# One encoder layer on one core: rows and attention outputs loaded by GpSimd, first loads of a scan by shares, a chain of small operations marked urgent

## The chip, the core and the metric

The kernel runs on one core of a Trainium2 chip. The metric is the time of one execution on the device in microseconds (us). TensorE (PE in the profile) does the matrix products, VectorE (DVE), ScalarE (ACT) and GpSimd (POOL) the elementwise work, and SyncE (SP) sends transfers; sixteen DMA engines carry them out.

## The reference

One layer of a bidirectional encoder is applied to two inputs with shared weights: a prompt of 1024 tokens (A in this document and in the names that end in `_a`) and a sample of 512 (B, `_b`), each 1024 wide, in float32.

- h = RMSNorm(x), and one product h @ w_in gives the columns for all that follows.
- The mLSTM branch has 4 heads of 256, with q and k after a short convolution and SiLU. In chunks of 128 positions, forwards and backwards, a state C is carried: num = (q k^T with decay weights) v + q C, and the head's output is num / max(|den|, exp(-m)). The two directions are added, normed by head and multiplied by two gates.
- The attention branch has 3 groups (window and dilation 128/1, 512/4, 2048/16) of 8 heads of 64. The groups' outputs are mixed by their softmax denominators and gated.
- merged = sigmoid(g_A) (y_A @ w_proj_m) + sigmoid(g_B) (y_B @ w_proj_a); out = merged @ w_out; y = x + RMSNorm(out).

## The kernel before

Every float32 operand is split into a rounded high part and the rest, the low part, and every product is three matmuls: high x high, low x high, high x low (lines 188 to 196 of the profile). A *dense step* is such a triple with 512 columns. A dense product (tile `dense`) is a unit of several steps into one PSUM bank; its weights come as a 512 KB load into one of two places (`wraw0`, `wraw1`), and are split by ScalarE (high, `wh`) and VectorE (low, `wl`).

The values and most projections of the prompt come first, up to 1056 us. From there on the rest of the dense units is the *fill*, laid between the steps of four stages whose own work has long chains of small operations:

1. the mLSTM of the prompt (`mlstm`, with `core` for one chunk's sums), from 1056 to about 1345 us,
2. the attention of the prompt (`attend`), to about 1655,
3. the mLSTM of the sample (`mlstm_short`), to about 1834, with the prompt's mix of the attention groups (`combine`) beside it,
4. the attention of the sample (`attend` again, with T.n = 4), to about 2122. Its fill is, among other things, `branches` and `final`: the merge and the output product of the prompt.

Then come the sample's `combine` with `final` of the prompt's second half, and the sample's `branches` and `final`.

A stage says how many fill steps go to one *share*; `fill(x)` issues x shares at that place in the program. TensorE's and SyncE's instructions run in the order in which the program writes them. Those of VectorE, ScalarE and GpSimd are put in an order by a scheduler, before the run, by what is ready and by priority; each engine then runs its own list strictly in order.

Nearly all transfers are sent by SyncE. Loads can be `queue`d; each `tick` of a stage sends `pace` of them, which `spread(n)` sets so that the queue is empty after n ticks; `need` sends all that are left of a group; `fetch` (line 229) sends a load at once, after the stores that it depends on; `flush` sends stores and weight loads that wait for their tick.

What the change touches:

- `core` (lines 949 to 1000): for each chunk and direction, a product `num` in PSUM; VectorE takes the maximum and the reciprocal (`r`); in the first half of the chunks ScalarE then writes `num` x `r` to the head's sums (`X` in the profile, L990), in the second half VectorE adds it (L993). That frees the bank for the next `num`.
- the start of `mlstm`: loads of Q, K and the gate rows, V and G at once, then `lead` = 4 shares of fill, then the first products `a` of Q and K (L892).
- `attend` for the sample: in each of 12 problems the next one's loads (q|k into Q0 and V1a, v, bias) are queued and spread over 3 ticks (T.n - 1).
- `split` (lines 1588 to 1604): the normed rows of a branch (`ym`), 128x512 each, 36 in all, go into five places in turn (`sraw`, `ymr0` to `ymr3`), and each is split by ScalarE (L1603) and GpSimd (L1604) into high and low part.
- `combine`: loads of the attention outputs (`og`, three groups for each of four row blocks of the sample, into V0a and V1a) and of the gate (`az`, into X1, Q0, az0, az1); VectorE computes the weights `cw` from the denominators (L1523 to L1533).
- `ot`: the places from which attention outputs are stored to `og`, six in the sample's attention.

GpSimd sends no transfer in this kernel. The kernel is built with `dynamic_dma_scratch_size=1024`.

Of the kernel before, what the change touches and what calls it, by code (L numbers as in the profile page):

```python
# [22 lines left out]
F32 = mybir.dt.float32  # L23
F32R = mybir.dt.float32r
AF = mybir.ActivationFunctionType
# [4 lines left out]
P = 128  # L30
# [145 lines left out]
class Net:  # L176
# [51 lines left out]

    def fetch(self, key, out, src):
        self.flush(lambda p: p[1] == key)  # L230
        return self.nc.sync.dma_start(out, src)

# [624 lines left out]
    def mlstm(self, T, fill, steps, first, banks, lead, after, beside=()):  # L857
# [10 lines left out]
        with ExitStack() as stack:  # L868
# [80 lines left out]
            def core(k):  # L949
# [23 lines left out]
                if i < n - 1:  # L973
                    e = P - 1 if d == 0 else 0
                    if i == 0:
                        cf = sb.tile([P, 2, 258], F32, name=f"cf{d}", bufs=1)
                        nc.vector.tensor_copy(cf, pc[:, :, :258])
                    else:
                        cf = C[d][0]
                        nc.vector.scalar_tensor_tensor(cf, cf, rw[:, 1, e:e + 1], pc[:, :, :258], op0=OP.mult, op1=OP.add)  # L980
                    ch = sb.tile([P, 2, 258], F32R, name=f"ch{d}", bufs=1)
                    cl = sb.tile([P, 2, 258], F32R, name=f"cl{d}", bufs=1)
                    nc.scalar.activation(ch, cf, AF.Copy)
                    nc.vector.tensor_sub(cl, cf, ch.bitcast(F32))
                    C[d] = (cf, ch, cl)
                r = sb.tile([P, 4], F32, name="r", bufs=4)
                nc.vector.tensor_scalar(r[:, 1:2], pn[:, 256:257], m["fl"], pn[:, 257:258], op0=OP.max, op1=OP.max)
                nc.vector.reciprocal(r[:, 2:3], r[:, 1:2])
                if i < n // 2:
                    nc.scalar.activation(hacc[:, c], pn[:, :256], AF.Copy, scale=r[:, 2:3])  # L990
                    return
                hs = hacc[:, c]
                nc.vector.scalar_tensor_tensor(hs, pn[:, :256], r[:, 2:3], hs, op0=OP.mult, op1=OP.add)  # L993
                hn = hn_of()
# [16 lines left out]
            def load_G(h):  # L1011
                for c in range(2):
                    self.queue(("G", h), ("G", S, 2 * h + c), G[:, c], T.G[2 * h + c])

            self.need(("qk", 0))
            for d in range(2):
                rows(0, d)
            self.need(("v", 0))
            load_G(0)
            fill(lead)  # L1020
            for _ in prepare(0):
# [82 lines left out]
    def mlstm_short(self, T, fill, steps, first, banks, lead, after, beside=()):  # L1104
# [11 lines left out]
        with ExitStack() as stack:  # L1116
# [10 lines left out]
            G = [x0[:, 2 * S * i:2 * S * (i + 1)].rearrange("p (c s) -> p c s", c=2) for i in range(2)]  # L1127
            fill.stage(steps, lead + 2 * len(rounds) + 3)

# [87 lines left out]
            weigh(1)  # L1217
            fill(1)
            next(beside, None)
# [212 lines left out]
    def attend(self, T, fill, steps, first, banks, outs, after=None, beside=None, at=()):  # L1432
# [5 lines left out]
        with ExitStack() as st:  # L1438
# [26 lines left out]
            for i in range(12):  # L1465
                now = coming
                for j, t in enumerate(now):
                    if j == 1:
                        if i < 11:
                            coming = ready(i + 1)  # L1470
                            self.spread(T.n - 1)
                        elif after:
                            after()
                            self.spread(T.n + 1)
                    self.tick()
                    if j == 0:
                        self.need(("att", i))
                    if j == 1:
                        self.need(("table", i))
                        self.later.pop(i, lambda: None)()  # L1480
                    tiles.append(t)
                    self.att_round(tiles, fill)
                    if len(tiles) in at:
                        next(beside, None)
# [18 lines left out]
    def combine(self, T, bank, cs, ys, sb, azs, slow):  # L1503
# [8 lines left out]
        def load(t):  # L1512
            for g in range(3):
                self.fetch(("og", T.S), cs[t % 2][:, g], T.og[g, :, t * P:(t + 1) * P].rearrange("h t w -> t h w"))

# [41 lines left out]

        load(0)
        yield
        az, w = {}, []  # L1560
        for t in range(T.n):
            az[t] = az_of()
            self.fetch(("az", T.S), az[t].rearrange("p (c s) -> p c s", c=4), T.az[:, :, t * P:(t + 1) * P].rearrange("c p s -> p c s"))
            if t + 1 < T.n:
                load(t + 1)
# [5 lines left out]
            if not slow:  # L1571
                yield
                yield
            if t > 0:
# [13 lines left out]
    def split(self, T, b, row, places, halves):  # L1588
# [6 lines left out]
        for i in range(m + 3):  # L1595
            if i < m:
                t = self.rows_in.pop(0)
                self.rows_in.append(t)
                got.append(t)
                self.fetch(("ym", T.S, min((row + i) // 2, 4)), t, T.ym[row + i, :, b * BLK:(b + 1) * BLK])  # L1600
            if i >= 3:
# [156 lines left out]
def body(tc, a):  # L1758
# [3 lines left out]
    with ExitStack() as st:  # L1762
# [192 lines left out]
        with ExitStack() as s1:  # L1955
# [36 lines left out]
            with ExitStack() as s2:  # L1992
# [4 lines left out]
                head = N.ml_load(A, 0)  # L1997
                N.mlstm(A, fill, STEPS[0], head, ("a", "num", "kv"), 4,
                        hold("qkv", lambda: N.att_first(A)))
# [24 lines left out]
            nc.sync.dma_start(N.postw, a["postw"][0:1].to_broadcast([P, D]))  # L2024
            N.attend(B, fill, STEPS[3], kept["qkv"], ("lg", "o", "pt"), 6)
            end = N.pool(s1, "end", 1, "right")
# [71 lines left out]
```

## Time and profile before

| | |
|---|---|
| runs | 2277.78 us median of 3 (2277.17 to 2277.89) |
| the profiled execution's own time | 2278.09 us |
| its span | 2276.3 us |
| granted TensorE clock over the span | 0.995 |
| busy: TensorE, VectorE, ScalarE, GpSimd | 98%, 64%, 48%, 27% of the span |
| moved by DMA | 425.05 MB, 187 GB/s on average |

A line of the profile names the engine, the line of the kernel, the operation and its tiles (output<-inputs, buffer numbers left out); what stands in brackets at its end is the idle time of that engine just before, and what ended it. "PEclk" is the clock that TensorE was granted, with 1.00 for full speed.

### The profile page before, as it was taken

How to read it: one execution, taken by the hardware profiler on the slowest of the kernel's cores; microseconds unless marked ns; L12 is line 12 of the kernel's file. 1: busy time of each engine (PE TensorE's matmuls, PEld its weight loads, DVE VectorE, ACT ScalarE, POOL GpSimd, SP SyncE). 2: the span in 40 equal slices, each digit the busy share in tenths (PEclk: the TensorE clock that was granted, in tenths of full speed). 3: DMA queues.
4: the chain of work that ended last, by engine and by line, in shares of the span. 5: the costliest groups of instructions: out<-in, count | busy, mean ns of one | idle time of the engine just before them, and what ended most of it. 6: DMA issues, size and time to landing. Idle time of an engine off the chain costs nothing. (4 is left out here: it accounts for less than half of the span.)

```text
span 2276.3 us, 35152 instructions
## 1 busy us (share of the span) xinstructions
PE 2235.5 (98%) x12210; PEld 1951.7 (86%) x12210; DVE 1467.8 (64%) x2777; ACT 1100.5 (48%) x2255; POOL 623.6 (27%) x801
## 2 busy tenths in 40 slices
PE   9999999999999999999999999999999999999998
PEld 9999998888887888887888889989888878888787
DVE  5587556767899655643787776675477744556563
ACT  7444223434444433334677766676644354544332
POOL 1000023333333322222567640001033321311311
PEclk9999999999999999999999999999999999999999
DMA  9556435555332223424666559988788888787673
GB/s 355 192 138 143 117 113 194 196 193 195 118 111 101 95 82 109 146 97 159 242 214 218 157 164 250 237 234 216 203 240 264 250 259 221 192 261 208 219 248 116
DMA packets 253627, 425.05 MB, mean 187 GB/s; under 512 B 26209, under 2 KB 150753, under 8 KB 252681
## 3 DMA queue, kind: packets, MB, share of 16 engines
q1 hardware_dynamic: 249848, 410.20, 58.7%
q10 hardware_dynamic: 3600, 12.59, 1.4%
q8 instruction: 97, 1.59, 0.3%
q14 instruction: 82, 0.66, 0.1%
HBM read 302.72 MB, written 128.37 MB: 189 GB/s over the span
## 5 line engine op out<-in xcount | busy, mean ns | idle before, releaser
L194 PE MATMUL dense<-H,wh 128*128 128x512 f32 x672 | 280.5, 417 | 0.0
L196 PE MATMUL dense<-H,wl 128*128 128x512 f32 x672 | 265.6, 395 | 0.5 <-DVE wl L253 0.5
L195 PE MATMUL dense<-H,wh 128*128 128x512 f32 x672 | 264.5, 394 | 0.0
L196 PE MATMUL d<-Hh,phla 128*128 128x512 f32 x608 | 237.4, 390 | 2.2 <-DVE phla L538 2.2
L194 PE MATMUL d<-Hh,phla 128*128 128x512 f32 x608 | 236.9, 390 | 0.0
L195 PE MATMUL d<-Hl,phla 128*128 128x512 f32 x608 | 236.8, 390 | 0.0
L195 PE MATMUL d<-vlo,Hh 128*128 128x322 f32 x704 | 220.4, 313 | 0.8 <-DVE vlo L384 0.8
L196 PE MATMUL d<-vhi,Hl 128*128 128x322 f32 x704 | 220.3, 313 | 0.0
L194 PE MATMUL d<-vhi,Hh 128*128 128x322 f32 x704 | 220.3, 313 | 0.0
L253 DVE TENSOR_TENSOR wl<-wraw,wh 128x1024 fp32r<-128x1024 f32 x109 | 137.0, 1257 | 89.8 <-ACT wh L252 87.7
L556 POOL TENSOR_TENSOR psum_w<-pw_raw 128x512 f32<-128x512 f32 x38 | 57.5, 1512 | 445.8 <-DMA pw_raw<-w_in 422.1
L1399 DVE CUSTOM_DVE_ANT_0 ls<-lg,bias 128x256 f32<-128x256 f32 (+1 forms) x288 | 93.7, 362 | 132.7 <-PE lg L1387 68.2
L194 PE MATMUL d<-Hh,phlb 128*128 128x512 f32 x456 | 177.6, 390 | 0.0
L196 PE MATMUL d<-Hh,phlb 128*128 128x512 f32 x456 | 177.6, 389 | 0.0
L195 PE MATMUL d<-Hl,phlb 128*128 128x512 f32 x456 | 177.6, 389 | 0.0
L1403 ACT ACTIVATE ls<-ls,nm 128x256 f32<-128x256 f32 (+1 forms) x288 | 129.9, 453 | 79.6 <-DVE nm L1401 63.1
L252 ACT ACTIVATE wh<-wraw 128x1024 fp32r<-128x1024 f32 x110 | 116.0, 1054 | 85.1 <-DMA wraw<-w_pm 32.8
L196 PEld LDWEIGHTS dense<-H,wl 128*128 128x128 f32 x672 | 126.7, 189 | 29.7 <-DVE wl L253 0.9
L195 PEld LDWEIGHTS dense<-H,wh 128*128 128x128 f32 x672 | 127.8, 190 | 13.6
L194 PEld LDWEIGHTS dense<-H,wh 128*128 128x128 f32 x672 | 127.4, 190 | 13.5
L196 PEld LDWEIGHTS d<-Hh,phla 128*128 128x128 f32 x608 | 114.1, 188 | 27.6 <-DVE phla L538 4.2
L195 PEld LDWEIGHTS d<-vlo,Hh 128*128 128x128 f32 x704 | 133.5, 190 | 1.5 <-DVE vlo L384 1.4
(556 smaller groups left out, 5722.2 us busy)
## 6 DMA issues: line engine op xcount, KB each, us to landing
pw_raw<-w_in SPq DMA_DIRECT2D x76, 512.0 KB
wraw<-w_in SPq DMA_DIRECT2D x76, 512.0 KB
aqk_a<-pwk SPq DMA_DIRECT2D x48, 512.0 KB
aqk_b<-sw SPq DMA_DIRECT2D x48, 256.0 KB
wraw<-w_pm SPq DMA_DIRECT2D x24, 512.0 KB
wraw<-w_out SPq DMA_DIRECT2D x24, 512.0 KB
vb<-w_vp SPq DMA_DIRECT2D x16, 644.0 KB
va<-w_vp SPq DMA_DIRECT2D x14, 644.0 KB
```

The costliest lines, as they stand in the source:

```text
L194: nc.tensor.matmul(out, lh, rh, start=start, stop=False)
L195: nc.tensor.matmul(out, lh, rl, start=False, stop=False)
L196: nc.tensor.matmul(out, ll, rh, start=False, stop=stop)
L252: self.splits = (nc.scalar.activation(hi[:, :n], raw[:, :n], AF.Copy), on.tensor_sub(lo[:, :n], raw[:, :n], hi[:, :n].bitcast(F32)))
L253: on.tensor_sub(lo[:, :n], raw[:, :n], hi[:, :n].bitcast(F32)))
L556: self.nc.gpsimd.tensor_add(s[:, 0], ws[1][:, 0], ws[1][:, 1])
L1399: nc.vector.tensor_tensor_reduce(out=ls[:, hh], in0=ts["lg"][hh], in1=bt[:, hh], scale=1.0, scalar=NEG, op0=OP.add, op1=OP.max, accum_out= ...
L1403: nc.scalar.activation(ls[:, hh], ls[:, hh], AF.Exp, bias=nm[:, hh:hh + 1], accum_out=ot[:, 128 + hh:129 + hh])
```

## The change

1. `fetch` can send on another engine's queue. The rows of `ym` in `split`, and the sample's `og` and `az` loads in `combine`, are sent by GpSimd: 36 + 12 + 4 = 52 loads leave SyncE.
2. The sample's `combine` sends the loads of its second row block at its very start, and those of block t + 2 after block t.
3. At the start of `mlstm` the weight load that waits for its tick is sent first, and V and G are no longer sent before the fill; `lead` is 6, and the six shares come one by one, each with a tick that sends some of the queued loads.
4. In `core` the maximum, the reciprocal and the operation that takes `num` out of its bank are marked as of high priority, and the low part of the state (`cl`) is issued after them.
5. `mlstm_short` has one more share, of fill ahead of its first sums.
6. In the sample's attention the loads of the second problem are all sent at one tick.
7. Ten places `ot` instead of six.

The number of instructions of every kind on every engine is the same but for the 52 loads. In the new file lines stand 1 to 14 lower (L990 of before is L991, L1604 is L1618, L1672 is L1686).

SyncE at the start of the sample's attention, before (Q0 and V1a take q and k of the next problem, `sraw` and `ymr` rows for `split`, `wraw` weights):

```order
L2024 DMA postw_18375<-postw 128x1024
L210 DMA wraw1_8707<-w_in 128x1024
L231 DMA sraw_8777<-ym_a_70 128x512
L231 DMA ymr0_18367<-ym_a_70 128x512
L231 DMA Q0_18005<-aqk_b_75 64x512 x2
L231 DMA V1a_18426<-aqk_b_75 64x512 x3
L210 DMA wraw0_8706<-w_pm 128x1024
L231 DMA ymr1_18368<-ym_a_70 128x512
L210 DMA wraw1_8707<-w_pm 128x1024
L231 DMA ymr2_18369<-ym_a_70 128x512
L231 DMA V1a_18426<-aqk_b_75 64x512
```

and now:

```order
L2038 DMA postw_18375<-postw 128x1024
L210 DMA wraw1_8707<-w_in 128x1024
L231 DMA Q0_18011<-aqk_b_75 64x512 x2
L231 DMA V1a_18430<-aqk_b_75 64x512 x4
L231 DMA Q0_18011<-aqk_b_75 64x512 x2
L231 DMA V1a_18430<-aqk_b_75 64x512 x4
L231 DMA bias2_8768<-erep_3048 128x256 x2
L210 DMA wraw0_8706<-w_pm 128x1024
```

All loads of the second problem now stand ahead of the next weights, and the rows are gone from this queue.

GpSimd at the end of the sample's attention, before (H3 are low parts of the merged rows `mg`, L1672; V1b and K1 those of the rows of the sample; `ss` is the norm of an output row):

```order
L1672 TENSOR_TENSOR H3_19607<-mg_20869,H2_19606 128x512
L1672 TENSOR_TENSOR H3_19607<-mg_20891,H2_19606 128x512
L1604 TENSOR_TENSOR V1b_20944<-ymr3_18370,V0b_20943 128x512
L1604 TENSOR_TENSOR V1b_20944<-sraw_8777,V0b_20943 128x512
L1672 TENSOR_TENSOR H3_19607<-mg_20931,H2_19606 128x512
L1604 TENSOR_TENSOR V1b_20944<-ymr0_18367,V0b_20943 128x512
```

and now:

```order
L1686 TENSOR_TENSOR H3_19611<-mg_20873,H2_19610 128x512
L231 DMA V1a_21083<-og_b_81 128x4x132 x2
L231 DMA Q0_21085<-az_b_77 128x4x128
L1686 TENSOR_TENSOR H3_19611<-mg_20895,H2_19610 128x512
L1618 TENSOR_TENSOR V1b_20948<-ymr3_18370,V0b_20947 128x512
L1618 TENSOR_TENSOR V1b_20948<-sraw_8777,V0b_20947 128x512
L1618 TENSOR_TENSOR V1b_20948<-ymr0_18367,V0b_20947 128x512
L1618 TENSOR_TENSOR V1b_20948<-ymr1_18368,V0b_20947 128x512
L1686 TENSOR_TENSOR H3_19611<-mg_20935,H2_19610 128x512
L1618 TENSOR_TENSOR K1_20950<-ymr2_18369,K0_20949 128x512
L231 DMA ymr3_18370<-ym_b_80 128x512
L231 DMA sraw_8777<-ym_b_80 128x512
```

The two loads into V1a wait until the last attention product has read it; the last two merged low parts and three row loads (the third, into `ymr0`, is the next row) stand behind them.

ScalarE in the prompt's mLSTM, at the second chunk, before (`rm` are decay weights, `qh`, `kh`, `ch` high parts, X the head's sums):

```order
L926 ACTIVATE rm_9174<-rm_9174,col1024_382 128x128
L926 ACTIVATE rm_9232<-rm_9232,col1024_382 128x128
L938 ACTIVATE qh_9186<-qw_9184 128x256
L983 ACTIVATE ch1_9161<-cf1_9035 128x516
L990 ACTIVATE X0_8806<-num_9079,r_9110 128x256
```

and now:

```order
L983 ACTIVATE ch0_9121<-cf0_9004 128x516
L926 ACTIVATE rm_9195<-rm_9195,col1024_382 128x128
L252 ACTIVATE wh0_8708<-wraw0_8706 128x1024
L991 ACTIVATE X0_8806<-num_9100,r_9124 128x256
L641 ACTIVATE sw2_8775<-dense_9000 128x512
```

X has left the second `rm` and two high parts behind it, and a weight split has come ahead of it.

The diff:

```diff
--- before.py
+++ after.py
@@ -226,9 +226,9 @@
         while any(g == group for g, _ in self.queued):
             self.fetch(*self.queued.pop(0)[1])
 
-    def fetch(self, key, out, src):
+    def fetch(self, key, out, src, queue=None):
         self.flush(lambda p: p[1] == key)
-        return self.nc.sync.dma_start(out, src)
+        return (queue or self.nc.sync).dma_start(out, src)
 
     def take(self, name, dt=F32R, cols=2048):
 
@@ -981,16 +981,21 @@
                     ch = sb.tile([P, 2, 258], F32R, name=f"ch{d}", bufs=1)
                     cl = sb.tile([P, 2, 258], F32R, name=f"cl{d}", bufs=1)
                     nc.scalar.activation(ch, cf, AF.Copy)
-                    nc.vector.tensor_sub(cl, cf, ch.bitcast(F32))
                     C[d] = (cf, ch, cl)
                 r = sb.tile([P, 4], F32, name="r", bufs=4)
-                nc.vector.tensor_scalar(r[:, 1:2], pn[:, 256:257], m["fl"], pn[:, 257:258], op0=OP.max, op1=OP.max)
-                nc.vector.reciprocal(r[:, 2:3], r[:, 1:2])
+                hs = hacc[:, c]
+                with self.tc.high_priority():
+                    nc.vector.tensor_scalar(r[:, 1:2], pn[:, 256:257], m["fl"], pn[:, 257:258], op0=OP.max, op1=OP.max)
+                    last = nc.vector.reciprocal(r[:, 2:3], r[:, 1:2])
+                    if i < n // 2:
+                        nc.scalar.activation(hs, pn[:, :256], AF.Copy, scale=r[:, 2:3])
+                    else:
+                        last = nc.vector.scalar_tensor_tensor(hs, pn[:, :256], r[:, 2:3], hs, op0=OP.mult, op1=OP.add)
+                if i < n - 1:
+                    with self.tc.issue_after(last.ins):
+                        nc.vector.tensor_sub(cl, cf, ch.bitcast(F32))
                 if i < n // 2:
-                    nc.scalar.activation(hacc[:, c], pn[:, :256], AF.Copy, scale=r[:, 2:3])
                     return
-                hs = hacc[:, c]
-                nc.vector.scalar_tensor_tensor(hs, pn[:, :256], r[:, 2:3], hs, op0=OP.mult, op1=OP.add)
                 hn = hn_of()
                 nc.scalar.activation(hn, hs, AF.Square, accum_out=r[:, 0:1])
                 nc.gpsimd.tensor_scalar(r[:, 1:2], r[:, 0:1], 16.0 / 256, 16 * EPS, op0=OP.mult, op1=OP.add)
@@ -1012,12 +1017,15 @@
                 for c in range(2):
                     self.queue(("G", h), ("G", S, 2 * h + c), G[:, c], T.G[2 * h + c])
 
+            self.flush(lambda p: p[1][0] == "w")
             self.need(("qk", 0))
             for d in range(2):
                 rows(0, d)
-            self.need(("v", 0))
             load_G(0)
-            fill(lead)
+            self.spread(lead)
+            for _ in range(lead):
+                self.tick()
+                fill(1)
             for _ in prepare(0):
                 fill(1 / 3)
             front(0)
@@ -1125,7 +1133,7 @@
             ym_of = Rot(self, [sb.tile([P, 256], F32, name=f"ym{i}", bufs=1) for i in range(3)])
             x0 = self.take("X0", F32)
             G = [x0[:, 2 * S * i:2 * S * (i + 1)].rearrange("p (c s) -> p c s", c=2) for i in range(2)]
-            fill.stage(steps, lead + 2 * len(rounds) + 3)
+            fill.stage(steps, lead + 2 * len(rounds) + 4)
 
             def rows(h):
                 for d in range(2):
@@ -1215,7 +1223,7 @@
             next(beside, None)
             front(0)
             weigh(1)
-            fill(1)
+            fill(2)
             next(beside, None)
             for k, (h, i) in enumerate(rounds):
                 self.tick()
@@ -1468,7 +1476,7 @@
                     if j == 1:
                         if i < 11:
                             coming = ready(i + 1)
-                            self.spread(T.n - 1)
+                            self.spread(T.n - 1 if i or T.n > 4 else 1)
                         elif after:
                             after()
                             self.spread(T.n + 1)
@@ -1511,7 +1519,8 @@
 
         def load(t):
             for g in range(3):
-                self.fetch(("og", T.S), cs[t % 2][:, g], T.og[g, :, t * P:(t + 1) * P].rearrange("h t w -> t h w"))
+                self.fetch(("og", T.S), cs[t % 2][:, g], T.og[g, :, t * P:(t + 1) * P].rearrange("h t w -> t h w"),
+                           None if slow else nc.gpsimd)
 
         by = lambda x: x.rearrange("p g (a b) -> p g a b", a=4)
 
@@ -1556,12 +1565,15 @@
             self.put(("ym", T.S, 4), T.ym[8:12, :, t * P:(t + 1) * P].rearrange("c p s -> p c s"), ya, az)
 
         load(0)
+        if not slow:
+            load(1)
         yield
         az, w = {}, []
         for t in range(T.n):
             az[t] = az_of()
-            self.fetch(("az", T.S), az[t].rearrange("p (c s) -> p c s", c=4), T.az[:, :, t * P:(t + 1) * P].rearrange("c p s -> p c s"))
-            if t + 1 < T.n:
+            self.fetch(("az", T.S), az[t].rearrange("p (c s) -> p c s", c=4), T.az[:, :, t * P:(t + 1) * P].rearrange("c p s -> p c s"),
+                       None if slow else nc.gpsimd)
+            if slow and t + 1 < T.n:
                 load(t + 1)
             for step in (lambda: w.append(weigh(t)), lambda: mix(t, w[t]), lambda: add(t)):
                 with self.tc.issue_after(self.splits[0].ins), self.tc.issue_after(self.splits[1].ins):
@@ -1570,6 +1582,8 @@
                     yield
             if not slow:
                 yield
+                if t + 2 < T.n:
+                    load(t + 2)
                 yield
             if t > 0:
                 turn(t - 1, az[t - 1])
@@ -1597,7 +1611,7 @@
                 t = self.rows_in.pop(0)
                 self.rows_in.append(t)
                 got.append(t)
-                self.fetch(("ym", T.S, min((row + i) // 2, 4)), t, T.ym[row + i, :, b * BLK:(b + 1) * BLK])
+                self.fetch(("ym", T.S, min((row + i) // 2, 4)), t, T.ym[row + i, :, b * BLK:(b + 1) * BLK], nc.gpsimd)
             if i >= 3:
                 t, (hi, lo), k = got.pop(0), halves[(i - 3) // 4], (i - 3) % 4
                 nc.scalar.activation(hi[:, k], t, AF.Copy)
@@ -1995,7 +2009,7 @@
                 sraw = sp.tile([P, BLK + 2], F32R, name="sraw")
                 N.sg, N.sraw = Rot(N, [sraw[:, :BLK]]), sraw.bitcast(F32)
                 head = N.ml_load(A, 0)
-                N.mlstm(A, fill, STEPS[0], head, ("a", "num", "kv"), 4,
+                N.mlstm(A, fill, STEPS[0], head, ("a", "num", "kv"), 6,
                         hold("qkv", lambda: N.att_first(A)))
                 with ExitStack() as s3:
                     lanes = N.lanes_short(B, N.pool(s3, "lane2", 1, "right"), lambda: N.bank("o").rearrange("p a b -> p (a b)"))
@@ -2022,7 +2036,7 @@
             N.xo_bufs = [(i, [N.osb.tile([P, BLK], F32, name=f"xo{i}{j}") for j in range(2)]) for i in range(2)]
             N.postw = N.osb.tile([P, D], F32, name="postw")
             nc.sync.dma_start(N.postw, a["postw"][0:1].to_broadcast([P, D]))
-            N.attend(B, fill, STEPS[3], kept["qkv"], ("lg", "o", "pt"), 6)
+            N.attend(B, fill, STEPS[3], kept["qkv"], ("lg", "o", "pt"), 10)
             end = N.pool(s1, "end", 1, "right")
             N.xo_bufs.insert(0, ("late", [end.tile([P, BLK], F32, name=f"xo2{i}") for i in range(2)]))
             with ExitStack() as s2:
```

## The prediction

> **What bounds the kernel now.** I read the page's busy times first, then the groups of waits of TensorE (columns: waiting engine, operation and line, what released it; total us, times, longest).
>
> ```profile
> PE 2235.5 (98%) x12210; PEld 1951.7 (86%) x12210; DVE 1467.8 (64%) x2777; ACT 1100.5 (48%) x2255; POOL 623.6 (27%) x801
> ...
> PE num L194 <- ACT X L990: 6.8, 6, 2.3
> PE lg L1387 <- DMA sraw<-ym_a: 4.7, 1, 4.7
> PE a L892 <- DMA K<-qk_a: 3.7, 2, 2.3
> ...
> PE dense L194 <- DVE mg L1716: 2.4, 1, 2.4
> ...
> PE num L196 <- POOL scl L1170: 1.1, 1, 1.1
> PE o L1422 <- ACT ot L1424: 1.1, 2, 0.7
> ...
> PE dense L196 <- POOL K L1672: 0.9, 1, 0.9
> ```
>
> TensorE sets the time: 98% busy. The change adds no matmul and takes none, so all it can win is idle time, in few places, and what idle time costs afterwards. That second cost is in the windows (columns: stretch, length, busy time of PE, PEld, DVE, ACT, POOL, then granted clock, DMA share, GB/s).
>
> ```profile
> 1056.00:1064.00 8.00, 8.00 (x36) 6.41 (x35) 5.08 (x8) 2.78 (x4) 0.44 (x8) 1.00 0.68 201
> 1068.20:1071.60 3.40, 3.23 (x16) 3.17 (x17) 0.00 (x0) 1.54 (x5) 2.42 (x5) 0.58 1.07 371
> 1098.90:1102.30 3.40, 3.40 (x15) 3.02 (x14) 1.35 (x3) 1.30 (x4) 1.46 (x4) 0.58 1.06 389
> 1290.10:1293.50 3.40, 3.40 (x15) 3.00 (x14) 2.31 (x5) 2.55 (x7) 1.05 (x2) 0.58 0.81 226
> 1856.70:1863.50 6.80, 3.15 (x10) 2.60 (x11) 2.77 (x7) 3.23 (x6) 3.74 (x5) 0.54 1.05 324
> 2143.40:2146.80 3.40, 3.39 (x9) 2.73 (x10) 3.40 (x14) 0.00 (x0) 0.00 (x0) 0.58 0.64 232
> ```
>
> Behind each of the five waits of 2.3 us or more the clock is down to 0.54 to 0.58 for 3.4 us, before it is back at 1.00. 3.4 us at 0.58 do the work of 2.0, so a wait of that size costs 1.4 us more than it lasts. The waits of 1.3 us and less have no such stretch. A wait need not vanish, then: under some 2 us its second cost goes.
>
> The Trainium skill (TensorE: Matmul & The Clock Gate, HAM oscillation) warns of TensorE gaps above about 3.4 us. The trace disagrees: a longest wait of 2.3 us was enough. By the page the three waits of 2.3 to 2.4 us would cost no clock and the sum below would be some 4 us smaller.
>
> **The first head of the long scan.** Dense steps (three matmuls) cover the loads of Q and K.
>
> ```profile
> 1045.80 2.42 POOL L253 TENSOR_TENSOR wl<-wraw,wh 128x1024 fp32r<-128x1024 f32 x1 [9.70 <-ACT wh L252]
> 1058.37 0.85 SPq L231 DMA_DIRECT2D K<-qk_a  x2
> 1063.76 0.39 PE L196 MATMUL dense<-H,wl 128*128 128x512 f32 x1
> 1065.62 0.49 PE L892 MATMUL a<-Q,K 128*128 128x128 f32 x2 [1.47 <-DMA K<-qk_a]
> 1068.37 2.97 PE L892 MATMUL a<-Q,K 128*128 128x128 f32 x14 [2.26 <-DMA K<-qk_a]
> ```
>
> Eleven steps end at 1064.15 and the products run from 1068.37 on. The written order now has seventeen: six more of 0.68 us (three matmuls 0.23 apart, as the 36 of 8 us in the first window) cover 4.1 of the 4.2 us. The steps are not extra work, only earlier. The third weight load moves ahead of Q and K on SP, but its place's last reader, GpSimd's split, ended at 1048.2, ten microseconds before K was sent, so I let K land where it did. Won: 3.4 us of the 3.73 (0.3 kept for slips) and 1.4 of clock, and half a microsecond because these weights are also earlier (the next such wait was 0.5): **5.3**. Bounds: 3.4 if the clock still drops, 6 if all goes.
>
> **The sums' chain in the scans.** Here ScalarE's order decides.
>
> ```profile
> 1095.10 0.40 ACT L926 ACTIVATE rm<-rm,col 128x128 f32<-128x128 f32 x1 [0.84 <-POOL rm L924]
> 1096.55 0.40 ACT L926 ACTIVATE rm<-rm,col 128x128 f32<-128x128 f32 x1 [1.05 <-POOL rm L924]
> 1097.16 0.62 ACT L983 ACTIVATE ch<-cf 128x516 fp32r<-128x516 f32 x1
> 1097.69 0.45 ACT L990 ACTIVATE X<-num,r 128x256 f32<-128x256 f32 x1
> ```
>
> X, for which TensorE waits 2.3 us, stood behind the second rm, which came late from GpSimd, and two more. In the new order it stands behind the first rm and one weight split (1.05 us): from 1095.50 that makes 1096.55, 1.1 us earlier. The gap is then 1.2, which draws no clock: 1.1 + 1.4 = **2.5**. Bounds: 0, if the split waits for its weights, and 3.7. The like wait at 1290 I leave as it is: there X still stands behind an rm, a head norm's copy and two splits, so being called urgent does not help. The subtraction that was put behind reciprocal is 0.6 us of a VectorE that is 64% busy: nothing.
>
> **The short scan.** Fill moved ahead of its first product is some four steps, 2.7 us, and covers the 1.1 us wait on scl and one of 0.3 before it: **1.4**.
>
> **Attention of the short sequence.** SP sent the second problem's loads in three portions.
>
> ```profile
> 1837.27 1.23 SPq L231 DMA_DIRECT2D Q<-aqk_b  x2
> 1854.11 1.09 SPq L231 DMA_DIRECT2D V1a<-aqk_b  x2
> 1855.11 0.48 PE L1387 MATMUL lg<-V1a,Q 128*128 128x256 f32 x2
> 1860.34 1.15 PE L1387 MATMUL lg<-V1a,Q 128*128 128x256 f32 x2 [4.74 <-DMA sraw<-ym_a]
> ```
>
> TensorE waits from 1855.6 for operands sent at 1854.11; the releaser named, sraw, is a row that SP sent just before. Now all fourteen go at once, from 1837 where the first portion began, and the rows are not in that queue. At 0.55 us each (1.09 for two) SP is through by 1845, ten microseconds before the product. The weight loads behind them go out some 3 us later; they are for units behind the one that TensorE takes up after this wait, which cover them. The wait of 4.74 goes, and of the 3.15 busy us at 0.54 another 1.5: **6.2**.
>
> Later the gates' copies on ScalarE were stuck behind rows that SP had sent late:
>
> ```profile
> 1965.89 0.63 ACT L1603 ACTIVATE H<-ymr 128x512 fp32r<-128x512 f32 x1 [4.16 <-DMA ymr<-ym_a]
> ```
>
> With rows sent as soon as a place is free, that goes; the waits on K (0.9) and ot (0.7) that follow are worth **1.5**, bounds 0 and 1.6.
>
> **The last combine.**
>
> ```profile
> 2134.25 1.60 SPq L231 DMA_DIRECT2D V1a<-og_b  x3
> 2141.61 0.17 DVE L1523 TENSOR_TENSOR cw<-V1a 128x8 f32<-128x8 f32 x1 [2.34 <-DMA V1a<-og_b]
> 2142.67 0.68 DVE L1716 TENSOR_TENSOR mg<-dense,postw 128x512 f32<-128x512 f32 x1
> ```
>
> VectorE stood at cw for V1a, and mg, which frees TensorE's bank, behind it. Two of these loads are now sent before 2110 and the third once the last outputs are stored. 2.4 + 1.4 of clock: **3.8**.
>
> Together 5.3 + 2.5 + 1.4 + 6.2 + 1.5 + 3.8 = 20.7 us.
>
> **What it costs: GpSimd becomes a queue.** It has 801 instructions, in order, and gets 52 loads between them, 16 of which read og or az in 512 pieces. No load is sent by GpSimd in this trace. The place where it matters is the end of the attention:
>
> ```profile
> 2101.81 0.28 PE L196 MATMUL lg<-V1a,Q 128*128 128x256 f32 x1
> 2101.09 1.81 POOL L1672 TENSOR_TENSOR H<-mg,H 128x512 fp32r<-128x512 f32 x1 [2.54 <-ACT H L1671]
> 2110.60 0.86 SPq L231 DMA_DIRECT2D ymr<-ym_b  x2
> 2110.82 1.27 POOL L1672 TENSOR_TENSOR H<-mg,H 128x512 fp32r<-128x512 f32 x1
> 2113.85 0.63 ACT L1603 ACTIVATE V0b<-ymr 128x512 fp32r<-128x512 f32 x1 [3.17 <-DMA ymr<-ym_b]
> 2119.98 0.60 ACT L1708 ACTIVATE sw<-dense 128x512 f32<-128x512 f32 x1
> 2120.70 0.69 DVE L1711 TENSOR_TENSOR sw<-dense,postw 128x512 f32<-128x512 f32 x1 [3.85 <-ACT sw L1708]
> 2121.51 0.47 PE L194 MATMUL dense<-Q,H 128*128 128x512 f32 x1
> ```
>
> In the new order two loads into V1a stand ahead of the last two merged low parts, and V1a is read until 2102.1. Behind them: the az load, seven subtractions of 1.27 (8.9 us), three row loads; the third row's copy now precedes, on ScalarE, the square of the dense tile whose bank TensorE takes up at 2121.51. With d the time a load holds GpSimd, the third row is sent by 2102.1 + 8.9 + 6d; 2.8 us from sending to copy (2111.05 to 2113.85), the copy 0.63, the square 0.60, the multiply 0.69, with 0.1 at the hand-overs: 2115.8 + 6d plus up to 1.3 of queueing between the engines, say 2117.1 + 6d, against 2121.4. Below d = 0.7 it is free. The eighth low part was just in time as well, and falls inside the same delay.
>
> Bounds for d: SP's 0.43 from below (0.86 for two); from above the whole landing, 2.8 for a row, and for og 5.8 (2135.8 to 2141.6). I take the nearest row on the same engine with the same tile, 1.27, for a row, and 2.0 for the loads in four times as many pieces (not four times 1.27, as SP's own og loads take 0.53 against 0.43). Then 3 x 2.0 + 3 x 1.27 = 9.8, less 4.3: 5.5, and 1.4 of clock, **6.9 lost**. Elsewhere GpSimd is 27% busy and the rows are a lap of five places ahead; in the short scan one row load stands before a head norm's power, which might lose 0.3.
>
> **Sum:** 2278.1 (the profiled run, 0.3 above the median of 2277.78) - 20.7 + 6.9 + 0.3 = 2264.6; against the median, **2264**.
>
> **Rivals.**
>
> *GpSimd held until its loads have landed (slower).* Mechanism: a load is not merely sent but holds GpSimd while it is moved. For it: the code reserves 1024 bytes for such loads, and the DMA engines are full where the clock rows show shares of 1.05. Against: nothing in a profile without such loads. Price: 3 x 5.8 + 3 x 2.8 = 25.8 - 4.3 + 1.4 = 22.9 at the end, 1.5 of the gates not won, and in attention B 32 row loads at 2.8 each before low parts, of which I let 5 us surface: 2278 - 20.7 + 22.9 + 1.5 + 5 = 2287. It is slower from a mean d of about 4 on.
>
> *VectorE delays the sending.* Something stretches GpSimd's work beside a VectorE that is 64% busy: the same subtraction took 1.81 us at 2101.09 and 1.27 at 2110.82. If sending is hit harder, each load could cost as much as its landing took, 2.8: 16.8 - 4.3 + 1.4 = 13.9 lost, 2271.
>
> The Trainium skill (SBUF — State Buffer, SBUF: two separate sides) calls this a trap: GpSimd cannot write the descriptors of its loads while VectorE holds the port they share, and 620 ns became 3100 beside a copy. By its 3.1 the sum would be 2273. No run shown here has such a load.
>
> *Urgency does not do what it says.* The scheduler's order is fixed before the run; if X's split waits for weights, the 2.5 are lost, and if the busier VectorE is as late at 1290 and 1098, another 1: 2268.
>
> *Loads on GpSimd are free.* d near SP's 0.43: nothing lost at the end, 2257.
>
> **Chances.** Forecast (2260 to 2267) 0.40, urgency 0.16, free loads 0.14, VectorE 0.14, held 0.16. A measurement of this kernel tells about 0.2%, 4.6 us, from no change, so faster ends at 2273.2. Faster: 0.40 + 0.16 + 0.14 and half of VectorE's, 0.77. Same, up to 2282.3: the other half and 0.03 of the held case, 0.10. Slower: 0.13. The range, 2254 to 2280, takes in free loads with X wholly won, and the VectorE case; most of the held case is left out. The likeliest case alone spans 2257 to 2270 (d from 0.4 to 2).
>
> **What would show it.** Right: no wait above 2 us on K, on the second lg, or on mg behind cw, clock 1.00 at those places, X earlier at the former 1098, and between the last lg and the end of attention a GpSimd whose sending takes 1 to 2 us a load, with a wait of TensorE for sw or mg of some 5 us there. Wrong: GpSimd's share much above 27%, low parts or rows waited for all along attention B; or K's loads landing later than 1068, in which case the six steps only move the wait.

## The result: slower, and the profile after

The changed kernel takes 2302.48 us (median of 4 runs, 2300.68 to 2304.18) against 2277.48 us before (4 runs): a ratio of 1.0113, 95% interval 1.0095 to 1.013. The forecast was 2264 us, faster; the time lies outside the range and on the other side.

The page of the changed kernel, part 1 and the waits of TensorE (columns as in the prediction):

```profile
span 2298.9 us, 35118 instructions
PE 2238.7 (97%) x12210; PEld 1956.2 (85%) x12210; DVE 1472.7 (64%) x2777; ACT 1102.8 (48%) x2255; POOL 649.9 (28%) x853
...
PE dense L194 <- DVE mg L1730: 12.9, 3, 6.0
PE dense L196 <- POOL H L1686: 6.5, 2, 4.6
PE o L1430 <- ACT ot L1432: 6.5, 2, 4.2
PE a L1211 <- ACT hn L1204: 5.2, 2, 4.1
```

The waits on K, on the second lg and on X at 1098 are gone, as forecast. The one on X at 1290, which was to stay, is down to 0.9 us, but TensorE now waits 2.3 us for VectorE's X at 1314. The four groups shown, two of them new and two grown from 2.4 and 1.1 us, take more than was won.

TensorE executes the same 12210 instructions in both kernels, nearly in the same order. So the time at which it comes to its n-th instruction, less the same time in the kernel before, shows where time went, stage by stage (us, from the traces; minus is ahead):

| instruction, and about where | changed | og on SP | rows on SP | 1792 bytes |
|---|---|---|---|---|
| 5000, before the first changed place | -0.7 | -1.4 | -1.3 | -2.4 |
| 7000, end of the long scan | -10.2 | -9.4 | -10.7 | -9.4 |
| 9000, end of the prompt's attention | -10.3 | -9.5 | -10.5 | -9.1 |
| 9400, in the short scan | -4.0 | -4.0 | -4.8 | -2.5 |
| 10200, start of attention B | -5.4 | -5.4 | -6.3 | -3.9 |
| 10600, in attention B | -2.1 | -4.3 | -7.3 | -1.5 |
| 11400, late in attention B | -4.0 | -6.1 | -6.3 | -3.7 |
| 11800, in the last combine | +21.1 | -6.4 | +17.4 | -5.5 |
| 12200, end | +22.3 | -6.4 | +17.4 | -3.1 |

The three columns on the right are experiments below. The row of instruction 5000 says how far to trust a difference: before anything is changed the traces already differ by up to 2.4 us.

The changed kernel won 10 us in the long scan, gave 5 back in the short one (6 by instruction 9400) and 1.4 in attention B (3 in its first part), and lost 26 at the end (11400 to the end of the table). That end on GpSimd (columns: start, duration, engine, line; in brackets idle time before, and what ended it; "issue" means that it waited for nothing that the profile shows):

```profile
2100.56 0.76 POOL L231 DMA_DIRECT2D V1a<-og_b  x1
2105.15 0.76 POOL L231 DMA_DIRECT2D V1a<-og_b  x1 [3.82 <-issue]
2108.70 0.75 POOL L231 DMA_DIRECT2D Q<-az_b  x1 [2.79 <-issue]
2109.46 1.27 POOL L1686 TENSOR_TENSOR H<-mg,H 128x512 fp32r<-128x512 f32 x1
...
2115.57 1.25 POOL L1686 TENSOR_TENSOR H<-mg,H 128x512 fp32r<-128x512 f32 x1
...
2118.01 0.57 POOL L231 DMA_DIRECT2D ymr<-ym_b  x1
2118.58 0.54 POOL L231 DMA_DIRECT2D sraw<-ym_b  x1
...
2162.53 0.76 POOL L231 DMA_DIRECT2D V0a<-og_b  x1 [3.45 <-issue]
...
2173.23 0.75 POOL L231 DMA_DIRECT2D V1a<-og_b  x1 [2.80 <-issue]
2173.99 0.59 POOL L1729 TENSOR_TENSOR ss<-ss,mhalf 128x1 f32<-128x1 f32 x1
```

A row load takes 0.54 to 0.57 us here and the next goes out at once. A load of og or az takes 0.75, but a further one right behind it stands 2.5 to 6.9 us before it goes out, and everything behind it on GpSimd stands with it. The landing times in the trace say what it stands for: in all twelve such places the next load goes out 0.30 to 0.37 us after the one before has landed. (The first load shown landed at 2104.84, 4.28 us after its start, and the second goes out at 2105.15.) What stood there: the seventh and eighth merged low parts, and the power of an output row's norm (`ss`, L1729). VectorE and TensorE, same trace:

```profile
2174.62 0.76 DVE L1733 SCALAR_TENSOR_TENSOR xo<-sw,ss,xo 128x512 f32<-128x512 f32 x1 [10.17 <-POOL ss L1729]
...
2177.88 0.68 DVE L1730 TENSOR_TENSOR mg<-dense,postw 128x512 f32<-128x512 f32 x1
```

```profile
2116.88 0.80 PE L196 MATMUL dense<-wh,H 128*128 128x512 f32 x1 [4.64 <-POOL H L1686]
2158.04 0.79 PE L194 MATMUL dense<-wh,H 128*128 128x512 f32 x1 [6.01 <-DVE mg L1730]
2178.62 0.80 PE L194 MATMUL dense<-V0b,wh 128*128 128x512 f32 x1 [5.51 <-DVE mg L1730]
```

VectorE waits 10.2 us for that power, and mg, which frees TensorE's bank, is queued behind. Each of these waits stands beside a stretch at half clock (0.50 in the 4 us from 2117, 2158 and 2178.6); the window of the second one (columns as in the prediction):

```profile
2158.00:2162.00 4.00, 3.96 (x9) 3.14 (x10) 1.78 (x3) 1.00 (x1) 0.75 (x1) 0.50 0.28 71
```

Over the whole span the clock is 0.990 against 0.995 before. By these two figures some 11 us of the loss are due to the clock, which is an estimate.

### The profile page after: what moved, and what is told of

The parts are those of the page before. It is cut to its first block, busy times and chain, and to the rows that moved or that the text cites. A ratio compares the mean times of both kernels' runs of the same rounds, so it can differ in the third digit from the quotient of the medians.

```text
span 2298.9 us, 35118 instructions
## 1 busy us (share of the span) xinstructions
PE 2238.7 (97%) x12210; PEld 1956.2 (85%) x12210; DVE 1472.7 (64%) x2777; ACT 1102.8 (48%) x2255; POOL 649.9 (28%) x853
## 5 line engine op out<-in xcount | busy, mean ns | idle before, releaser
L195 PEld LDWEIGHTS d<-Hl,phla 128*128 128x128 f32 x608 | 114.1, 188 | 23.7
```

The source lines that it names most:

```text
L195: nc.tensor.matmul(out, lh, rl, start=False, stop=False)
```

## The experiments

Three theories of the loss: **ring**, the descriptors of an og load fill the space reserved for them, so that the next load waits until there is room again; **rows**, any load on GpSimd does it; **held**, GpSimd or its loads are slow for another reason (landing, VectorE). Then each part alone. Every run is compared with runs of the kernel before on the same chip.

**1. og and az back on SP, rows stay on GpSimd.**

```diff
-    T.og[g, ...], None if slow else nc.gpsimd)     # az likewise
+    T.og[g, ...])                                  # az likewise; load(1), load(t + 2) as before the change
```

> The changed kernel with the last combine as before: its attention outputs and gates are sent by SyncE again, in the old order; the rows stay on GpSimd. Ring theory (a load in 512 pieces finds the queue of descriptors full and holds GpSimd until the one before has drained, 2.5 to 5.8 us each, and the norm's powers behind it make VectorE and TensorE wait): the waits at 2111 to 2190 go, TensorE is at the end of attention B some 4 us ahead of the kernel before and stays there, 2272 to 2276 us. Rival (any load on GpSimd does it, rows too): most of the loss stays, above 2290 us.

2272.81 us against 2276.03; ratio 0.9994, interval 0.9985 to 1.0004. The loss of 25 us between instructions 11400 and 11800 is gone. Rows on GpSimd are not the cause of it. The ratio is within what can be told from no change, so the medians 3 us apart say nothing.

**2. Rows back on SP, og and az stay on GpSimd.**

```diff
-    T.ym[row + i, :, b * BLK:(b + 1) * BLK], nc.gpsimd)
+    T.ym[row + i, :, b * BLK:(b + 1) * BLK])
```

> The changed kernel with the 36 row loads on SyncE again; attention outputs and gates stay on GpSimd. Ring theory: the end of the kernel still loses over 20 us against the kernel before, 2293 to 2303 us in all. Rival (the rows do it): below 2280 us.

2295.5 us, ratio 1.0083 (1.0067 to 1.0098). The loss at the end stays, 23.7 us between instructions 11400 and 11800 by the table. In attention B, where the changed kernel fell back, this one does not: -6.3, -7.3, -6.3.

**3. 1792 bytes for descriptors instead of 1024, nothing else.**

```diff
-    dynamic_dma_scratch_size=1024
+    dynamic_dma_scratch_size=1792
```

> The changed kernel with 1792 instead of 1024 bytes reserved for the descriptors of GpSimd's loads, and nothing else: three loads of 512 pieces fit where one did. Ring theory: the idle time of GpSimd between two such loads falls from 2.5 to 5.8 us to below 1 us, the 10 us waits of VectorE for the norm's power go, and the time falls by 12 to 22 us, to 2280 to 2290 us. Rival (GpSimd is held until its loads have landed, or VectorE delays the writing of descriptors): the idle time stays and the time too, 2298 to 2306 us.

2277.98 us, ratio 1.0008 (0.9998 to 1.0017): 24.5 us below the changed kernel's median, a little more than expected. Every engine has the same instructions in the same order as in the changed kernel. GpSimd in this run:

```profile
2099.20 1.52 POOL L231 DMA_DIRECT2D V1a<-og_b  x2
2100.70 0.75 POOL L231 DMA_DIRECT2D Q<-az_b  x1
...
2125.18 1.63 POOL L231 DMA_DIRECT2D az<-az_b  x2 [1.35 <-DVE wl L253]
...
2140.50 2.33 POOL L231 DMA_DIRECT2D V0a<-og_b  x3 [3.53 <-DVE X L1550]
2142.86 0.93 POOL L1728 TENSOR_SCALAR ss<-ss 128x1 f32<-128x1 f32 x1
2145.54 0.81 POOL L231 DMA_DIRECT2D V1a<-og_b  x1 [1.74 <-DVE X L1557]
2146.78 1.62 POOL L231 DMA_DIRECT2D V1a<-og_b  x2 [0.44 <-issue]
```

Three loads now go out in 2.3 us without a pause. The groups of V1a loads, first in the changed kernel, then in this one (busy us, mean ns, idle before):

```profile
L231 POOL DMA_DIRECT2D V1a<-og_b x6 | 4.6, 762 | 17.3 <-issue 17.3
```

```profile
L231 POOL DMA_DIRECT2D V1a<-og_b x6 | 4.6, 764 | 2.3 <-DVE X L1557 1.7 <-issue 0.4
```

The sending itself is the same, 0.76 us; the idle time that the profile could not name falls from 17.3 to 0.4 us. What is left is the same wait one step later: three loads are out, and a fourth goes out 0.3 us after the oldest of them has landed, whatever releaser the view names. (The load at 2120.15 landed at 2124.85, and the fourth, counted from it, goes out at 2125.18; the one at 2140.50 landed at 2145.23, and the fourth goes out at 2145.54.) This settles it for the ring: one number was changed, and with it the count of loads that may be out at once. It is the landing of an earlier load that ends the wait, as the rival had it, but for want of room. The Trainium skill (DMA: Bandwidth & Descriptors, Terms) gives a descriptor 16 bytes, written to rings for GpSimd's loads. By it an estimate, on the assumption, which no run here shows, that the reserved bytes are the room for one DMA engine: 1024 bytes are 64 descriptors; a load of 512 pieces spread over sixteen engines is 32 on each, and two loads with any end mark do not fit; 1792 bytes are 112, three loads. The traces agree: one load out before the hold at 1024 bytes, three at 1792.

**4. Only what needs no load on GpSimd, without the short scan's share.** The edits of 1 and 2 together, and `fill(1)` and `+ 3` as before in `mlstm_short`.

> Only the parts without GpSimd loads and without the short scan's extra share: the first head's loads by shares with lead 6, the sums' chain marked urgent, the second problem's loads at one tick, ten output places. By my terms for these parts (5.3 + 2.5 + 6.2 = 14 us): 2264 us. By what the changed kernel showed (10 us ahead at the end of the first scan, 4 to 5 us lost again at two waits on output places in attention B): 2266 to 2272 us. If the order that the scheduler made for the scan costs in places that are not marked: above 2272 us.

2267.85 us, ratio 0.9964 (0.9951 to 0.9977): 8.2 us faster than before, in the expected part that allowed for new waits on output places.

**5. The new start of the long scan alone.**

```diff
+            self.flush(lambda p: p[1][0] == "w")
-            self.need(("v", 0))
-            fill(lead)                      # lead 4
+            self.spread(lead)               # lead 6
+            for _ in range(lead):
+                self.tick()
+                fill(1)
```

> The kernel before with the new start of the first scan alone: weights first, lead 6, V and G by shares. My term: 5.3 us faster, bounds 3.4 and 6, 2271 us; the waits of products on K (3.7) gone. Rival (the steps only move the wait, or the scheduler's new order gives it back later in the scan): within 2 us of before at the end of the scan.

2269.08 us against 2277.71, ratio 0.9964 (0.995 to 0.9978), 8.2 us: more than the 5.3 forecast, though 5.3 lies inside the interval. The products no longer wait for K, and the wait on X at 1098 is gone as well, which I put down to the other order that the scheduler made.

**6. Urgency alone** (the `core` part of the diff).

> The kernel before with the sums' chain marked urgent and the state's low part behind it, alone. My term: 2.5 us faster by the wait on X at 1098, the one at 1290 unchanged, 2274 us. By the changed kernel (the waits of 2.3 on X at both places down to 0.9, and a new wait of 2.3 for VectorE's X at 1314): about 4 us ahead through most of the scan, 1 to 4 at its end.

2273.58 us, ratio 0.9982 (0.9972 to 0.9992), 4.1 us. The wait at 1098 is gone; the one at 1290 is as long as before, though this time the clock behind it stays at 1.00 (1283.8 to 1287.2):

```profile
1283.83 0.39 PE L194 MATMUL num<-V1a,sch 128*128 128x258 f32 x1 [2.34 <-ACT X L991]
```

**7. The second problem's loads at one tick alone.**

> The kernel before with the second problem's loads of the sample's attention at one tick, alone. My term: 6.2 us faster, 2270 us. Rival, from the new waits on an output place at 1857 and 1881 in the changed kernel (ScalarE's copy stands behind a weight split whose weights come late because the fourteen loads were sent first): 2 to 3 us of it come back, 2273 us; if those waits came from GpSimd's early rows instead, they are not here.

2274.05 us, ratio 0.9987 (0.9974 to 1.0): 3.0 us by the ratio, half of the 6.2 forecast, with an interval that just reaches no change. The wait on lg is gone; the trace has 5.6 us of waits on an output place (1.1 before). The trace is of an execution of 2279.42 us, above this kernel's median, so no more is read from it alone.

**8. One more share in the short scan, alone.**

> The kernel before with the one more share of fill ahead of the short scan's first sums, alone. My term: 1.4 us faster. Rival, from the changed kernel's wait of 4.1 us for a head's norm at 1676 (the fill reaches the next unit's weights before they are loaded, and VectorE's split of them stands ahead of the norm's chain): 3 to 6 us slower, 2279 to 2283 us.

2274.54 us, ratio 0.9984 (0.9971 to 0.9996). Alone it does not cost what the changed kernel lost there; the wait on scl is gone. Its trace ends only 0.4 us ahead of before, so the gain rests on the times alone.

**9. As 1, without that share.**

> The changed kernel with the last combine as before and without the short scan's extra share; the rows stay on GpSimd. Beside the run that differs only in that share (2272.8 us, waits of 4.2 and 1.1 us for a head's norm at 1677 and 1700): if the share is what costs there, these waits fall to below 2 us together and the time is 5 to 6 us lower, 2267 us. If the shift of the whole fill by the longer lead, or the one row load ahead of a norm's power, is what costs, the waits stay, 2272 us.

2271.68 us, ratio 0.9975 (0.9964 to 0.9985). TensorE in run 1 and in this one:

```profile
1677.07 0.69 PE L1211 MATMUL a<-ident,hn 128*128 128x128 f32 x2 [4.20 <-ACT hn L1204]
```

```profile
1675.55 0.44 PE L1211 MATMUL a<-ident,hn 128*128 128x128 f32 x2 [1.66 <-ACT hn L1204]
```

Between instructions 9000 and 9400 run 1 loses 5.5 us and this run 1.0; run 3 and the same kernel without the share (run 10) show it again, 6.6 and 0.8. So the share does cost there, but only with the rest. That the fill is then far enough ahead to need weights that are not in yet is how I read the traces; it was not measured by itself. In the changed kernel (ScalarE, and VectorE behind it):

```profile
1668.06 1.06 ACT L252 ACTIVATE wh<-wraw 128x1024 fp32r<-128x1024 f32 x1 [1.94 <-DMA wraw<-w_in]
```

```profile
1669.15 1.23 DVE L253 TENSOR_TENSOR wl<-wraw,wh 128x1024 fp32r<-128x1024 f32 x1 [0.28 <-ACT wh L252]
...
1670.90 0.16 DVE L1195 RECIPROCAL r<-r 128x1 f32<-128x1 f32 x1
```

The split of late weights stands ahead of the reciprocal that the head's norm needs. The medians of runs 1 and 9 differ by only 1.1 us, not by the 5 to 6 expected. They were taken on two chips, whose times for the kernel before differ by 1.8 us; by their ratios the two are some 4 us apart. In its trace run 9 also lost 2.4 us more in the long scan, where its program is the same up to the scheduler's order.

**10. The whole change, 1792 bytes, without the share.**

> The whole change, with 1792 bytes for descriptors and without the short scan's extra share. If my account of the loss is complete (24 us by the descriptors, 6 by the share): 2270 to 2273 us, faster than before by 0.2 to 0.3%.

2275.59 us, ratio 0.9994 (0.998 to 1.0008): not told from no change, 2.6 to 5.6 us above what was expected. My account of the loss was not complete. The trace shows where it fails: this run is 9.6 us ahead of before at instruction 11800 and 5.2 at the end. In between, at 2171, TensorE waits to transpose (`tp`) mixed rows X of the sample, which stand behind a weight split on VectorE, and half clock follows (columns as for the waits before):

```profile
PE tp L1562 <- DVE X L1557: 2.7, 1, 2.7
```

The three kernels with 1792 bytes and early og loads (runs 3, 10 and 11) wait 1.9 to 2.7 us there and lose 2.1 to 4.4 us between these instructions. Those that send og by SyncE lose nothing there. What makes X late was not tested.

**11. The same with the rows on SP.**

> As the run before, with the rows sent by SyncE: only the attention outputs and gates are sent by GpSimd, 1792 bytes for descriptors, no extra share. If GpSimd's early rows crowd out the weights in attention B (a wait of 4.6 us on an output place at 1881 with them, 2.1 without): 2 to 4 us below the run with the rows on GpSimd, 2265 to 2268 us. Beside the run with no load on GpSimd at all (2267.9 us) it shows what early loads for the last combine are worth: 0 to 3 us.

2272.2 us, ratio 0.9967 (0.9952 to 0.9982): 3.4 us below run 10, as expected, but 4 to 7 us above the time that was expected. In attention B, ScalarE of the changed kernel, of run 10 and of this run:

```profile
1880.34 1.06 ACT L252 ACTIVATE wh<-wraw 128x1024 fp32r<-128x1024 f32 x1 [7.80 <-DMA wraw<-w_pm]
1881.30 0.26 ACT L1432 ACTIVATE ot<-o 128x128 f32<-128x128 f32 x1
```

```profile
1875.49 1.06 ACT L252 ACTIVATE wh<-wraw 128x1024 fp32r<-128x1024 f32 x1 [7.15 <-DMA wraw<-w_pm]
```

```profile
1873.12 1.06 ACT L252 ACTIVATE wh<-wraw 128x1024 fp32r<-128x1024 f32 x1 [3.00 <-DMA wraw<-w_pm]
```

The copy of an attention output (ot) stands behind a split whose weights come late; TensorE waits 4.2 us with rows on GpSimd (4.1 in run 10) and 1.7 without. This wait is 2.9 to 4.6 us in the five kernels with rows on GpSimd, and 1.3 to 3.0 in the five others that send the fourteen loads at one tick. That rows sent early take room on the DMA engines from these weights fits, and was not measured by itself. Beside run 4 (ratio 0.9964) early og loads on GpSimd show no gain.

**12. As 4, without urgency.**

> The start of the first scan by shares, the second problem's loads at one tick and ten output places, without urgency and without any load on GpSimd. Alone the first was worth 8.6 us, the second 3.7, urgency 4.1; with all three it was 8.2. If urgency and the new start win the same waits twice, this is as fast as with urgency, 2267 to 2269 us against 2277; if urgency still adds its own, 2270 to 2272 us.

2269.98 us against 2280.05, ratio 0.9964 (0.995 to 0.9978), the same ratio as with urgency: the new start and urgency win the same waits. From instruction 5000 to the end of the long scan the trace wins 9.2 us without urgency and that of run 4 wins 8.8 with it, so urgency adds nothing there that shows once the start is in. Of the whole change the start of the long scan is what pays; it alone has this ratio too. (Each ratio is good to about 3 us, so a remainder of that size stays open.)

## Why the prediction was wrong

**The step that failed** is the cost of GpSimd's loads. It was worked out for one place, the end of the attention, and all else was covered by "Elsewhere GpSimd is 27% busy". By the times of TensorE's instructions the changed kernel loses 8.8 us at the place that was priced (6.9 forecast, 11520 to 11580) and 19.8 us behind it (11680 to 11780), where nothing was put down: there each further og load waits until the one before has landed, and the powers of the norms wait with it.

**What bounds the kernel** was right: TensorE, and idle time in few places. The waits named as gains on K, on X at 1098, on scl and on the second lg are gone. That half clock stands behind every wait of 2.3 us or more, and behind none below "some 2 us", holds in the trace before and not in all the others. A wait of 2.98 us in run 2 (it ends at 1877.2) has a clock of 1.00 in the 3.4 us behind it, and one of 1.39 us in run 4 (it ends at 1851.8) has 0.51 from 1853.2 to 1856.6. In the fourteen traces every wait above 3.4 us has half clock beside it, and shorter ones from 1.3 us on have it or not. So the 1.4 us that several terms add for the clock may or may not fall due.

**The first head** (5.3 forecast): right in its mechanism. The products begin at 1067.34 without a wait, so K had landed by then. It came out larger, 8.2 alone; the wait on X at 1098 went with it, as the order behind it changed too.

**Urgency** (2.5): alone 4.1, the wait at 1290 unchanged as said. But the sum added it to the first head's term, and the two overlap; together they gave 8 to 10, which is near the 7.8 of the sum by luck.

**The short scan** (1.4): the sign failed. The step assumed that fill moved ahead costs nothing, and did not ask which weights the moved fill then needs, and what VectorE has behind their split. With the rest of the change it lost some 5 us; alone it lost nothing (run 8).

**Attention B** (6.2 + 1.5): the wait on lg went, but the clause that the weights "are for units behind the one that TensorE takes up after this wait, which cover them" failed: TensorE was covered, ScalarE's in-order queue was not, and output copies stand in it. Of the 7.7 us nothing stayed: between instructions 10200 and 11400 the changed kernel even falls back by 1.4. The traces of all ten kernels with the fourteen loads at one tick lie between 1.5 us won and 2.2 lost there. The waits on rows did fall: ScalarE waits 9 to 15 us for rows over the whole kernel in the five with rows on GpSimd and 31 to 38 in the nine without. ScalarE does not bound the kernel, and no time shows it. Even so the first of the two long waits on an output place has a row behind it; the copy (ot) at 1856.98 stands behind this one and two weight splits:

```profile
1851.74 0.63 ACT L1617 ACTIVATE K<-ymr 128x512 fp32r<-128x512 f32 x1 [5.97 <-DMA ymr<-ym_a]
```

**The last combine** (3.8 forecast): the wait on mg behind cw falls from 2.4 to 1.4 us, without half clock, and the changed kernel wins 4.1 us there (11620 to 11680). But mg waits 1.4 us as well in kernels that send og by SyncE in the old order (runs 4, 5 and 12), so the early loads are not shown to be what won it.

**The cost of GpSimd's loads** decided the result. The price of d was split the wrong way. For a row I took 1.27; it is 0.55, below the point (0.7) at which it is free. For og I took 2.0 from how SP's loads of both kinds compare; it is 0.76 to send and 2.5 to 6.9 before the next one can go, around the upper bound of 5.8 that I had and set aside. At the priced place the two errors nearly cancel: the six loads hold GpSimd 8.9 us for og and az and 1.7 for rows, 10.6 in all against 9.8. That is luck. The wait came on the low parts themselves, and not on sw or mg as forecast. And I priced one place only. Sixteen such loads stand in GpSimd's order up to 2173, and the powers of the norms behind the last eleven cost more (waits of 6.0 and 5.5) than the merged low parts at 2111 and 2117 (1.9 and 4.6). An average of GpSimd's busy time said nothing of them.

**The rivals.** "Held until its loads have landed" had the right effect and named the reserved 1024 bytes, and its size at the end was near (22.9 forecast for six loads at one place, 26 measured over all of the end, so by luck). Its mechanism, a load that holds GpSimd while it is moved, was only half right: nothing is held after a row load, and compute runs right behind an az load (2109.46) and an og load (2173.99). It is the next large load that waits, for room, and at 1024 bytes room comes when the one before has landed. "VectorE delays the sending" fell: 0.54 to 0.84 us for each of the 52 loads, though VectorE is 64% busy; what the Trainium skill (SBUF — State Buffer, SBUF: two separate sides) warns of did not show here. That "urgency does not do what it says" was true at 1290, not at 1098.

Open: how much of what attention B gave back is the rows and how much the fourteen loads; what makes X late behind early og loads; and the share of the scheduler's order in the 2 us by which equal programs differ at the end of the long scan.

## What to carry to other kernels

Before loads are given to GpSimd, count their pieces against the space reserved for descriptors: here one load that filled it made the next one wait for its landing, and with it every small operation queued on that engine. A price for a new queue has to be followed through all that stands behind it up to the end, not at the place first looked at. Work moved ahead pulls its own loads ahead too; ask what the engines that prepare those have behind them in their queues.

## What was not expected of the hardware

Loads on GpSimd are cheap to send, 0.55 us for 128 rows of 2 KB and 0.76 us for 512 pieces of 528 bytes, against 0.43 and 0.53 on SP; their price was in the room for descriptors, and 768 bytes more of it were worth 24 us. The profile shows that wait as idle time with "issue" as its end, or under a releaser that came earlier. What tells it is that the load goes out 0.3 us after an earlier one has landed.
